# Three unused memory tiles shift where the operands of the weight products begin

## The chip, the core and the metric

The kernel runs on one core of a Trainium2 chip. The metric is the device time of one execution in microseconds (us), the median of several runs. The engines are named as in the profile: PE is TensorE with its matmuls, PEld its weight loads, DVE is VectorE, ACT is ScalarE, POOL is GpSimd, SP is SyncE, which issues the loads of the weights.

## What is computed

Two transformer blocks in float32 over 256 tokens with 1024 features, cut to what matters here:

```python
for l in range(DEPTH):                       # first block
    h = rmsnorm(x, norm_mix[l])
    proj = h @ w_in[l]
    ...                                      # two attention mixers: o_a, o_b
    mix = (jax.nn.sigmoid(gate_a) * (o_a @ w_branch_a[l])
           + jax.nn.sigmoid(gate_b) * (o_b @ w_branch_b[l]))
    x = x + mix @ w_out[l]
    h = rmsnorm(x, norm_mlp[l])
    x = x + jnp.square(jax.nn.relu(h @ w_mlp_in[l])) @ w_mlp_out[l]
...
for l in range(DEPTH):                       # second block
    f = swiglu(rmsnorm_2(x, ffn1_pre_g[l]), ffn1_w_gate[l], ffn1_w_up[l], ffn1_w_down[l])
    x = x + 0.5 * rmsnorm_2(f, ffn1_post_g[l])
    y = hybrid_mixer(...)                    # w_in_2, attention and mLSTM, w_out_2
    x = x + rmsnorm_2(y, mix_post_g[l])
    f = swiglu(rmsnorm_2(x, ffn2_pre_g[l]), ffn2_w_gate[l], ffn2_w_up[l], ffn2_w_down[l])
    x = x + 0.5 * rmsnorm_2(f, ffn2_post_g[l])
```

Nearly all arithmetic is in the products with the weight matrices. The mixers add small products, softmaxes and scans.

## The kernel before

**Products in three parts.** Every operand of a weight product is split into a high part (rounded to float32r, the one-pass float32 format of TensorE) and a low part (the rest). A product is then three matmuls: high by high, high by low and low by high. The activations live in pairs of tiles (`xh` and `xl`, `hT0` and `hT1`, `mT`, `mT2`, `mlT`, `attT`, `oaT`, `obT`), the weights in `hi` and `lo`.

**Stream of the weights.** `plan` lists all weight matrices in units of two k-tiles by up to 512 columns. `stream_dma` loads a unit into one of four `raw` buffers through SP's queue, five units ahead of its use. `stream_split` makes `hi` on ACT (line 249) and `lo` on DVE (line 250), two units ahead, into four buffers each. `load_unit` hands a unit to the product.

**Two forms of product.** A matmul has a stationary operand, of which 128 columns are loaded into the array (a weight load, PEld), and a moving operand, whose columns then stream through. The profile names the moving one first: `acc<-xh,hi` has `xh` moving and `hi` stationary.

- `gemm_feat` (lines 332, 334 and 335): 128 columns of the weights are stationary and all 256 tokens of the activations are moving. This is used for everything that gives features by rows: `w_in`, gate and up matrices, `w_mlp_in`, the branches.
- `gemm_tok` (lines 288, 289 and 290): 128 tokens of the activations are stationary and a whole weight row is moving, 512 columns, or 386 and 352 in two pieces of the `w_in` matrices. This is used for the down products (`hT`), the output products (`mT`, `mT2`) and the values.

Between the k-tiles of a product, `flush` issues small work of the mixers on PE. The order on ACT, DVE and PE comes from the scheduler, that on POOL and SP is the order of the code.

**Two places where another engine leads.** In the first mixer, `bias_job` writes a table to memory and reads it back through POOL's queue into `BT` (lines 554 to 561), and POOL then clears `gek` (line 716), for which the compressed keys wait. In the second mixer, `qkdone` sends each of six query and key pieces through two transfers and three POOL operations on 32 rows (lines 1212 to 1216), one piece behind the other, and the attention starts behind the last.

**Where the tiles lie.** Pools are laid out one behind the other from the left end of each partition, others from the right. Ahead of the large tiles lie a reserved piece of 16,384 bytes, four small constants of 128 bytes together, `ident` (512 bytes), `cols` (544) and `ones` (512): 18,080 bytes, which is 32 past a multiple of 128. All that follows inherits the 32. The small tiles of pool `st` end at 96 past such a multiple, and what follows them has 96, and so have most tiles of the right side. By the program's allocation, the operands of weight products begin as follows (bytes within a partition; in brackets, past a multiple of 128):

| tile | before | after the change |
|---|---|---|
| `xh`, `xl` | 34464, 42656 (32) | 34816, 43008 (0) |
| `hi`, first of four | 67232 (32) | 67584 (0) |
| `lo`, first of four | 83616 (32) | 83968 (0) |
| `hT0` | 110048 (96) | 110592 (0) |
| `mT0`, `mlT0` | 212960 (96) | 210944 (0) |
| `attT0` | 127712 (96) | 128256 (0) |
| `oaT0` | 177888 (96) | 178432 (0) |

Inside a tile, the slices that one matmul takes are 512 bytes apart (128 columns of the weights or tokens), 1024 (one k-tile of the activations), 2048 (one k-tile of 512 weight columns), or 1544 and 1408 (one k-tile of 386 and 352 columns).

Of the kernel before, what the change touches and what calls it, by code (L numbers as in the profile page):

```python
# [9 lines left out]
F32 = mybir.dt.float32  # L10
# [6 lines left out]
PSUM = bass.MemoryType.PSUM  # L17
DRAM = bass.MemoryType.DRAM
SIDE_R = "right"
# [9 lines left out]
FF2 = 2816  # L29
VIF = 386               # a quarter of the columns of the values, input and forget gates  # L30
SPLIT_AHEAD = 2         # weight units split ahead of their use
DMA_AHEAD = 5           # and loaded ahead of it


# ---------------------------------------------------------------- host layout
def widths_of(n):
# [3 lines left out]
class Wt:  # L40
    """A weight matrix cut into units of KT k-tiles by up to 512 columns, each unit contiguous."""

# [76 lines left out]

# constants of shape alone, [128, n] each  # L120
CONSTS = {}
# [73 lines left out]

# ---------------------------------------------------------------- the program
class Prog:
# [6 lines left out]

    # ---- weights
    def plan(self):
        """The order in which the column chunks of the weights are used."""
        o = [(W_IN1, c) for c in (4, 0, 1, 3, 2, 5, 6, 7, 8)]
        for c in range(2):
            o += [(W_BRB, c), (W_BRA, c)]  # L210
        o += [(W_OUT1, 0), (W_OUT1, 1)]
        o += [(W_MI, c) for c in range(8)] + [(W_MO, 0), (W_MO, 1)]

        def ffn(g, u, d):
            r = []
            for c in range(len(FFW)):
                r += [(g, c), (u, c)]
            return r + [(d, 0), (d, 1)]
        o += ffn(W_G1, W_U1, W_D1)
        o += [(W_IN2, c) for c in (6, 0, 1, 2, 3, 4, 5, 7, 8, 9, 14, 15, 16, 17, 10, 18, 12, 19, 11, 13, 20, 21)]  # L220
        o += [(W_ATT, 0), (W_ATT, 1), (W_MLB, 0), (W_MLB, 1), (W_OUT2, 0), (W_OUT2, 1)]
        o += ffn(W_G2, W_U2, W_D2)
        return [(W, c, u) for W, c in o for u in range(len(W.off[c]))]

    def stream_dma(self, upto):
        """Loads of the weights, up to a unit of the plan."""
        nc = self.nc
# [9 lines left out]
    def stream_split(self, upto):  # L237
        """High and low parts of the weights, up to a unit of the plan."""
        nc = self.nc
# [21 lines left out]

    # ---- work that waits for a place between the products
    def later(self, *fs):
# [10 lines left out]
    def gemm_tok(self, W, c, xh, xl, done, head=0, tail=0, mid=None, late=None, rate=1, delay=0, acc=None):  # L274
        """Token-major: accumulators [128 tokens, width], one per token tile; done(t, acc) when one is complete.
        In the first `head` and the last `tail` units token tile 0 goes ahead of tile 1; mid() comes before tile 1
        at the head, late(n) after each k-tile of tile 1 at the tail, n of them left."""
        nc = self.nc
# [41 lines left out]
    def gemm_feat(self, W, c, xh, xl, done, rate=1, delay=0):  # L320
        """Feature-major: accumulators [128, 2 feature tiles, 256 tokens]; done(i, acc)."""
        nc = self.nc
# [17 lines left out]

    # ---- small helpers
    def ptr(self):
# [14 lines left out]
    def split_one(self, src, k, ts, hi, lo, gcol=None, scale=None):  # L357
        """src(t, k) [128 tokens, 128], for the token tiles ts, transposed into hi/lo[:, k, :]."""
        nc = self.nc
# [14 lines left out]
    def split_T(self, src, ks, ts, hi, lo, gcol=None):  # L374
        """One job for the tensor engine per k-tile."""
        def job(k):
            return lambda: self.split_one(src, k, ts, hi, lo, gcol)
        return [job(k) for k in ks]
# [5 lines left out]
    def held(self, on):  # L384
        """What is traced inside queues behind the last split of activations, if `on`."""
        es = ExitStack()
        if on:
            for i in self.mark:
                es.enter_context(self.tc.issue_after(i.ins))
        return es  # L390

    def ssq(self, acc, src, scale=1.0):
        """acc [128,1] = sum of squares of src [128, n]."""
        nc = self.nc
# [4 lines left out]
    def newton_rsqrt(self, y, v, n, name):  # L399
        """y = v ** -0.5 on DVE."""  # L400
        nc = self.nc
# [12 lines left out]

    # ---- whole
    @contextmanager
    def banks(self, acc, tr, sm=0, o=0):
        """The PSUM banks of a phase."""
        with ExitStack() as es:
# [14 lines left out]
    def run(self):  # L434
# [9 lines left out]
        with ExitStack() as es:  # L444
# [16 lines left out]
            self.cols = self.cp.tile([128, 136], F32, name="cols")  # L461
            self.ones = self.cp.tile([128, 128], F32, name="ones")
            nc.scalar.dma_start(self.cols, ap["cols"])
            for c in range(4):
# [22 lines left out]
    def rows_rms(self, x, name):  # L487
        """Reciprocal root mean square of the rows of x: [128, 2]."""
        s = self.small(2, name + "_s")
# [8 lines left out]
    def along_free(self, rs, name):  # L498
        """rs [128, 2] by token laid along the free axis of every partition: [128, 256]; and the job for it."""
        nc = self.nc  # L500
# [10 lines left out]

    # ---- block 1: mixers
    def block1_mix(self, x0, x):
        tc, nc, ap, g = self.tc, self.nc, self.ap, self.g
        with ExitStack() as es, ExitStack() as rs_:
# [4 lines left out]
            ip = rpool("idx", 2)  # L520
            # keeps the tensor engine's clock up while the first loads are under way
            ps = self.psm()
# [13 lines left out]

            # position bias: BT[p, h, j] = table[bucket(128 + p - j), h], masked where the distance is negative
            tot = sum(CONSTS[n].shape[1] for n in C1)
# [8 lines left out]
            def bias_job():  # L547
# [3 lines left out]
                nc.vector.tensor_tensor(tv, ps[:16, :384], neg, op=ALU.add)  # L551
                # copies of the table in DRAM, read back with a shift by one from row to row
                tvd = self.dp.tile([16, 16, 384], F32, name="tvd")
# [8 lines left out]

            # projections
            qi = cp.tile([128, 2, 256], F32, name="qi")
# [46 lines left out]

            # indexer and top-k mask
            M = cp.tile([128, 2, 256], F32, name="M")
# [75 lines left out]

            # compressed keys and values  # L690
            kcT = cp.tile([128, 2, 16], F32, name="kcT")         # block diagonal over the two groups
            nc.gpsimd.memset(kcT, 0.0)
# [51 lines left out]

            # attention
            lp = rpool("att", 4)
# [18 lines left out]
            units = []  # L765
            for br in (1, 2, 0):        # 0: DSA; 1: slc; 2: win
                for t in (1, 0):
# [12 lines left out]
            def bm(U):  # L780
                """Position bias and top-k mask of a DSA unit's heads."""
                t, nh, h0 = U["t"], U["nh"], U["heads"][0]
# [55 lines left out]

            # compressed branch
            Lc = cp.tile([128, 2, 8, 16], F32, name="Lc")  # L840
# [70 lines left out]

            # gates
            gate = cp.tile([128, 16, 256], F32, name="gate")
# [52 lines left out]

    # ---- block 1: MLP, and the final norm
    def mlp(self, x1):
# [57 lines left out]
    def split_sb(self, h, hT, k):  # L1026
        """h [128, 2, 256] in SBUF into k-tiles k, k + 1 of hT."""
        nc = self.nc
# [27 lines left out]
    def down_post(self, W, hT, gi, x, mul, name, rs=None, gcol=None):  # L1056
        """x + mul * rmsnorm(h @ W * rs) * gain; starts on the transposed operand of the next layer (gain gcol)."""
        nc, tc = self.nc, self.tc
# [26 lines left out]
        def done0(t, ps):  # L1085
            square(0, t, ps)
            gained(0, t, ps)
            # loads the square root's table ahead of its use
            nc.scalar.activation(st[t][:, 3:4], sq[:, t:t + 1], AF.Sqrt)
# [58 lines left out]

    # ---- block 2: mixer
    def mixer2(self, x):  # L1150
        tc, nc, ap, g = self.tc, self.nc, self.ap, self.g
        xT, js = self.nextT
        with ExitStack() as es, ExitStack() as rs_:
# [40 lines left out]

            # attention projections
            qkp = rpool("qk", 1)
# [6 lines left out]
            def qkdone(i, gr):  # L1203
                def f(j, ps):
# [3 lines left out]
                    if j == 0:  # L1208
                        return
                    # rotation of the first 32 rows  # L1210
                    sw = rp.tile([32, 4, 256], F32, tag="sw", name="sw")
# [5 lines left out]
                return f  # L1217
            # input and forget gates of the mLSTM
            gif = gp.tile([128, 2, 8], F32, name="gif")
# [69 lines left out]

            # attention  # L1290
            lp = rpool("att2", 3)
# [67 lines left out]

            # values with a column of ones per head, and gates  # L1360
            mp = pool("ml", 1)
# [24 lines left out]

            # conv + silu on q and k of the mLSTM (feature-major)
            cw = self.cols[:, 56:120].rearrange("p (f j) -> p f j", f=16)
# [131 lines left out]

# ---------------------------------------------------------------- launch
# [14 lines left out]
```

## Time and profile before

| what | value |
|---|---|
| time, median of 3 runs | 1155.5 us (1154.68 to 1156.64) |
| profiled execution, first to last instruction (span) | 1152.0 us |
| mean granted TensorE clock | 0.992 |
| PE busy | 1125.9 us, 98% of the span |
| PEld busy | 1044.8 us, 91% |
| DVE, ACT, POOL busy | 732.2, 553.8 and 137.1 us |
| moved by the DMA engines | 197.03 MB, 171 GB/s in the mean |

The profiled execution has no other time than its span on record; the median of the runs lies 3.5 us above it, which is taken as what lies around the span. A busy PE means that a matmul is under way. It doesn't say how fast columns stream, since a matmul's end is modelled and neighbours overlap. What tells the pace is the distance from one matmul's start to the next one's.

### The profile page before, as it was taken

The numbers are of one execution on the slowest core, as the hardware profiler recorded it, in microseconds if no ns is written. First come the engines' busy times: TensorE is split into PE (matmuls) and PEld (weight loads), VectorE is DVE, ScalarE is ACT, GpSimd is POOL, SyncE is SP. The second block draws the span as 40 slices with busy tenths as digits, with TensorE's granted clock in tenths as the row PEclk, the third lists the DMA queues.
The fourth block names the chain that finished last, engine by engine and source line by source line (L and its number), as shares of the span: only waits on it lengthen the run. The fifth ranks groups of instructions, "written<-read, shape, count | busy, mean of one in ns | idle before, by whom it ended". The sixth has DMA issues, their size and how long they took to land.

```text
span 1152.0 us, 19495 instructions
## 1 busy us (share of the span) xinstructions
PE 1125.9 (98%) x7808; PEld 1044.8 (91%) x7808; DVE 732.2 (64%) x1155; ACT 553.8 (48%) x818; POOL 137.1 (12%) x141
## 2 busy tenths in 40 slices
PE   8988999999999999999999998999999999999997
PEld 8887899899988899999888998889999989999986
DVE  5755676766654466655547677556779776656553
ACT  6324454455544455444446334545555556444442
POOL 0411230000000000000000676000323000000000
PEclk9998999999999999999999999999999998999999
DMA  8783114555555556554654655444545565554662
GB/s 291 251 170 108 67 57 147 185 183 186 182 188 191 182 183 197 179 184 158 216 169 167 200 185 161 163 129 146 183 147 165 166 193 157 190 182 157 210 187 79
DMA packets 57035, 197.03 MB, mean 171 GB/s; under 512 B 6828, under 2 KB 7100, under 8 KB 56688
## 3 DMA queue, kind: packets, MB, share of 16 engines
q1 hardware_dynamic: 53856, 186.44, 49.4%
q0 software_dynamic: 2800, 9.21, 3.5%
q8 instruction: 61, 1.00, 0.3%
q14 instruction: 30, 0.25, 0.1%
q10 hardware_dynamic: 288, 0.14, 0.0%
HBM read 192.84 MB, written 1.44 MB: 169 GB/s over the span
## 4 chain that ended last, share of the span: by engine, by line
PE 85%; POOL 5%; DMA 4%; DVE 4%; issue 1%; ACT 1%; DVEq 0%; POOLq 0%; ACTq 0%
PE acc L332 16%; PE acc L334 16%; PE acc L335 16%; PE acc L290 9%; PE acc L289 9%; PE acc L288 9%; POOL sw L1215 2%; PE sm L795 2%; DMA sw<-qkT 2%; POOL qkT L1216 2%; DMA BT<-tvd 2%; PE o L828 1%; DVE lo L250 1%; POOL qkT L1214 1%; PE o L1337 1%
## 5 line engine op out<-in xcount | busy, mean ns | idle before, releaser
L250 DVE TENSOR_TENSOR lo<-raw,hi 128x1024 fp32r<-128x1024 f32 (+3 forms) x364 | 450.4, 1239 | 304.7 <-ACT hi L249 302.8
L249 ACT ACTIVATE hi<-raw 128x1024 fp32r<-128x1024 f32 (+3 forms) x364 | 372.9, 1025 | 452.8 <-PE acc L334 242.6
L332 PE MATMUL acc<-xh,hi 128*128 128x256 f32 x1656 | 471.1, 286 | 0.6 <-ACT hi L249 0.3
L334 PE MATMUL acc<-xl,hi 128*128 128x256 f32 x1656 | 471.3, 285 | 0.0
L335 PE MATMUL acc<-xh,lo 128*128 128x256 f32 x1656 | 469.4, 285 | 0.1
L332 PEld LDWEIGHTS acc<-xh,hi 128*128 128x128 f32 x1656 | 317.7, 192 | 4.5 <-issue 3.0
L334 PEld LDWEIGHTS acc<-xl,hi 128*128 128x128 f32 x1656 | 318.7, 192 | 2.4 <-issue 2.0
L335 PEld LDWEIGHTS acc<-xh,lo 128*128 128x128 f32 x1656 | 317.6, 192 | 1.6 <-issue 1.0
L290 PE MATMUL acc<-hi,hT 128*128 128x512 f32 x304 | 120.4, 396 | 0.0
L289 PE MATMUL acc<-lo,hT 128*128 128x512 f32 x304 | 120.2, 395 | 0.0
L288 PE MATMUL acc<-hi,hT 128*128 128x512 f32 x304 | 119.7, 396 | 0.0
L289 PEld LDWEIGHTS acc<-lo,hT 128*128 128x128 f32 x304 | 57.2, 188 | 13.7
L290 PEld LDWEIGHTS acc<-hi,hT 128*128 128x128 f32 x304 | 57.2, 188 | 13.7
L288 PEld LDWEIGHTS acc<-hi,hT 128*128 128x128 f32 x304 | 57.0, 188 | 13.4
L288 PE MATMUL acc<-hi,xh 128*128 128x386 f32 (+1 forms) x128 | 48.2, 378 | 0.9 <-ACT xh L366 0.9
L289 PE MATMUL acc<-lo,xh 128*128 128x386 f32 (+1 forms) x128 | 47.5, 371 | 0.0
L290 PE MATMUL acc<-hi,xl 128*128 128x386 f32 (+1 forms) x128 | 46.9, 372 | 0.2 <-DVE xl L367 0.2
L1034 POOL DMA_DIRECT2D row<-in_rows x4 | 2.3, 574 | 295.7 <-DVE xf L1017 216.8
L806 ACT ACTIVATE L<-L,nn 128x256 f32<-128x256 f32 (+1 forms) x48 | 21.2, 443 | 25.8 <-DVE nn L804 22.4
L288 PEld LDWEIGHTS acc<-hi,xh 128*128 128x128 f32 x128 | 24.0, 188 | 4.4 <-ACT xh L366 1.3
L290 PEld LDWEIGHTS acc<-hi,xl 128*128 128x128 f32 x128 | 24.0, 188 | 3.7 <-DVE xl L367 0.8
L289 PEld LDWEIGHTS acc<-lo,xh 128*128 128x128 f32 x128 | 24.1, 189 | 2.3
(414 smaller groups left out, 1263.1 us busy)
## 6 DMA issues: line engine op xcount, KB each, us to landing
raw<-in_w_in SPq DMA_DIRECT2D x100, 512.0 KB, 3.6
raw<-in_ffn_w_down SPq DMA_DIRECT2D x44, 512.0 KB, 4.4
raw<-in_ffn_w_gate SPq DMA_DIRECT2D x40, 512.0 KB, 3.5
raw<-in_ffn_w_up SPq DMA_DIRECT2D x40, 512.0 KB, 3.5
raw<-in_w_mlp_in SPq DMA_DIRECT2D x32, 512.0 KB, 3.5
raw<-in_w_mlp_out SPq DMA_DIRECT2D x32, 512.0 KB, 3.4
raw<-in_w_out SPq DMA_DIRECT2D x16, 512.0 KB, 3.6
raw<-in_w_in SPq DMA_DIRECT2D x16, 386.0 KB, 3.1
```

The source lines that it names most:

```text
L249: nc.scalar.activation(hi[:, :n * w], raw[:, :n * w], AF.Copy)
L250: nc.vector.tensor_tensor(lo[:, :n * w], raw[:, :n * w], hi[:, :n * w], op=ALU.subtract)
L288: nc.tensor.matmul(ps[t][:, :w], xh[:, k, sl], hi, start=(k == 0), stop=False)
L289: nc.tensor.matmul(ps[t][:, :w], xh[:, k, sl], lo, start=False, stop=False)
L290: nc.tensor.matmul(ps[t][:, :w], xl[:, k, sl], hi, start=False, stop=last)
L332: nc.tensor.matmul(o, hi[:, fs], xh[:, k, :], start=(k == 0 and f % 2 == 0), stop=False, skip_group_check=True)
L334: nc.tensor.matmul(o, hi[:, fs], xl[:, k, :], start=False, stop=False, skip_group_check=True)
L335: nc.tensor.matmul(o, lo[:, fs], xh[:, k, :], start=False, stop=last, skip_group_check=True)
L795: nc.tensor.matmul(ps[:, i, :], q[pr:pr + 64, U["fts"][i], t * 128:t * 128 + 128], kk, start=True, stop=True)
L806: nc.scalar.activation(L[:, i, :], L[:, i, :], AF.Exp, bias=nn[:, i:i + 1], scale=1.0, accum_out=lsum[:, t, br, h:h + 1])
L1215: nc.gpsimd.tensor_tensor(sw, sw, bc4(1), op=ALU.mult)
L1216: nc.gpsimd.tensor_tensor(q[0:32], q[0:32], sw, op=ALU.add)
```

## The change

Three tiles are added that nothing writes or reads: 352 bytes per partition behind `ones` in pool `const`, 2016 bytes at the right end in a pool of its own, and 192 bytes at the head of pool `st`. The first makes 18,080 bytes into 18,432, nine times 2048. The third brings the end of `st` to a multiple of 2048. The second moves all tiles of the right side. No instruction is added, removed or moved on any engine; only buffer numbers and addresses differ. The rest of the diff removes comments and docstrings.

```diff
@@ -460,6 +460,10 @@
             self.ident = self.cp.tile([128, 128], F32, name="ident")
             self.cols = self.cp.tile([128, 136], F32, name="cols")
             self.ones = self.cp.tile([128, 128], F32, name="ones")
+
+            self.cp.tile([128, 88], F32, name="pad_l")
+            pool("padr", 1, side=SIDE_R).tile([128, 504], F32, name="pad_r")
+            self.small(48, "pad_s")
             nc.scalar.dma_start(self.cols, ap["cols"])
             for c in range(4):
                 nc.sync.dma_start(x0[:, 2 * c:2 * c + 2, :], ap["xT"][:, 2 * c:2 * c + 2, :])
```

The second k-tile of a 386-column unit begins 1544 bytes into its tile, which is 8 past a multiple of 128 in both kernels when counted from the tile's start.

## Rows read from the trace of the kernel before

**Rows 1.** The page's shares of the chain of work that ended last, by engine.

```profile
PE 85%; POOL 5%; DMA 4%; DVE 4%; issue 1%; ACT 1%; DVEq 0%; POOLq 0%; ACTq 0%
```

**Rows 2.** The view of waits, of PE: who was waited for, us in total, times, longest us.

```profile
PE sm L726 <- DVE gek L717: 9.0, 1, 9.0
PE sm L1307 <- POOL qkT L1216: 3.0, 1, 3.0
```

**Rows 3.** PE's timeline in a stretch that holds only feature products from `xh` and `xl`: start in us, length, line, operands (the moving one first), shapes. Sixty-four intervals lie between the first and the last row.

```profile
251.80 0.28 PE L334 MATMUL acc<-xl,hi 128*128 128x256 f32 x1
251.92 0.28 PE L335 MATMUL acc<-xh,lo 128*128 128x256 f32 x1
...
259.48 0.28 PE L335 MATMUL acc<-xh,lo 128*128 128x256 f32 x1
```

**Rows 4.** The same of feature products from `mlT`. Twenty-two intervals lie between the first and the last row.

```profile
904.23 0.28 PE L334 MATMUL acc<-mlT,hi 128*128 128x256 f32 x1
...
906.83 0.28 PE L335 MATMUL acc<-mlT,lo 128*128 128x256 f32 x1
```

**Rows 5.** The same of a down product from `hT`: sixty-two intervals from the first row to the last.

```profile
329.72 0.39 PE L288 MATMUL acc<-hi,hT 128*128 128x512 f32 x1
329.95 0.40 PE L289 MATMUL acc<-lo,hT 128*128 128x512 f32 x1
...
344.19 0.39 PE L290 MATMUL acc<-hi,hT 128*128 128x512 f32 x1
```

**Rows 6.** The same of a value product of 512 columns from `xh`: four intervals from the first row to the last.

```profile
724.08 0.39 PE L288 MATMUL acc<-hi,xh 128*128 128x512 f32 x1
...
724.99 0.39 PE L289 MATMUL acc<-lo,xh 128*128 128x512 f32 x1
```

**Rows 7.** The same of a value product of 386 columns: six intervals from the first row to the last.

```profile
713.49 0.34 PE L289 MATMUL acc<-lo,xh 128*128 128x386 f32 x1
...
714.53 0.34 PE L289 MATMUL acc<-lo,xh 128*128 128x386 f32 x1
```

**Rows 8.** PE's timeline, two merged rows of small matmuls in plain float32, in which a moving column takes two cycles: twelve with 128 moving columns, and two with 257. The length runs from the first one's start to the last one's end.

```profile
753.92 1.50 PE L1337 MATMUL o<-v,PT 128*128 128x128 f32 x12
...
848.85 0.59 PE L1454 MATMUL o<-vm,w 128*128 128x257 f32 x2
```

**Rows 9.** The duration of a single one of these, by tile: count, ns (least, median, most), first and last start, forms.

```profile
L1337 PE MATMUL o<-v,PT x72: 270/275/377, 742.2 to 789.3; 128*128 128x128 f32 x72
...
L1454 PE MATMUL o<-vm,w x8: 377/378/380, 843.2 to 895.8; 128*128 128x257 f32 x8
```

**Rows 10.** PE's matmuls by line and form: operands, shapes, count, then busy us and mean ns of one, then idle time before them. The two other lines of each product have the same counts.

```profile
L332 PE MATMUL acc<-xh,hi 128*128 128x256 f32 x1648 | 469.1, 286 | 0.6 <-ACT hi L249 0.3 <-DVE x L959 0.2
...
L288 PE MATMUL acc<-hi,hT 128*128 128x512 f32 x304 | 119.7, 396 | 0.0
...
L288 PE MATMUL acc<-hi,xh 128*128 128x512 f32 x64 | 25.7, 401 | 0.0
...
L288 PE MATMUL acc<-hi,mT 128*128 128x512 f32 x64 | 25.3, 398 | 0.0
...
L288 PE MATMUL acc<-hi,xh 128*128 128x386 f32 x64 | 22.5, 355 | 0.9 <-ACT xh L366 0.9
```

**Rows 11.** The other feature products, from the view of line 332: operands, count, ns of one (least, median, most), first and last start, forms.

```profile
L332 PE MATMUL acc<-mlT,hi x64: 278/279/365, 903.4 to 926.6; 128*128 128x256 f32 x64
...
L332 PE MATMUL acc<-obT,hi x32: 279/279/363, 186.0 to 203.6; 128*128 128x256 f32 x32
...
L332 PE MATMUL acc<-oaT,hi x32: 279/279/363, 192.4 to 209.2; 128*128 128x256 f32 x32
...
L332 PE MATMUL acc<-attT,hi x32: 278/279/281, 890.8 to 903.1; 128*128 128x256 f32 x32
```

**Rows 12.** The chain that ended last in order of time, the ends of two stretches: start us, us, what.

```profile
62.51 6.29 DMA tvd<-tv
...
72.98 17.57 DMA BT<-tvd
634.81 5.13 DMA sw<-qkT
...
708.39 2.95 POOL qkT L1216
```

**Rows 13.** The instructions of line 332 in these two stretches: length, busy PE and PEld with counts, granted clock, DMA share, GB/s.

```profile
62.50:91.80 29.30, 10.78 (x37) 6.99 (x37) 0.88 0.92 172
634.80:711.30 76.50, 43.61 (x155) 29.57 (x154) 1.00 0.59 185
```

**Rows 14.** The view of waits, of ACT: us in total, times, longest us.

```profile
ACT hi L249 <- PE acc L334: 242.6, 140, 5.2
ACT hi L249 <- PE acc L290: 130.8, 83, 4.5
```

**Rows 15.** The splits of a full unit, by line and form.

```profile
L250 DVE TENSOR_TENSOR lo<-raw,hi 128x1024 fp32r<-128x1024 f32 x324 | 407.8, 1261 | 277.9 <-ACT hi L249 276.3 <-PE sm L363 0.5 <-PE acc L334 0.2
L249 ACT ACTIVATE hi<-raw 128x1024 fp32r<-128x1024 f32 x324 | 343.0, 1059 | 413.1 <-PE acc L334 218.1 <-PE acc L290 119.1 <-issue 48.9
```

**Rows 16.** The page's list of loads: tile and source, queue, count, KB each, median us to landing.

```profile
raw<-in_ffn_w_gate SPq DMA_DIRECT2D x40, 512.0 KB, 3.5
```

**Rows 17.** PE in a stretch of feature products alone: length, busy us of PE with count, granted clock, DMA share, GB/s.

```profile
250.00:300.00 50.00, 50.00 (x419) 1.00 0.58 190
```

## The prediction, made before the change was run

> **What bounds the kernel now.** I read the chain of work that ended last first: 85% of it is PE, and POOL and DMA have 9% together [rows 1]. PE's own waits are next: two are over a microsecond long and matter here, 9.0 us behind a POOL clear and 3.0 us behind a POOL rotation [rows 2]. So the time is PE's pace, except in two stretches that another engine leads. In order of time the chain shows these: a table's way through memory from 62.5 us until its last piece lands at 90.5, and six rotations one behind the other from 634.8 to 711.3 [rows 12].
>
> The pace is the distance between matmul starts. In a stretch of feature products it is (259.48 - 251.80) / 64 = 120.0 ns, the same from one row to the next [rows 3], at a granted clock of 1.00, the 2.4 GHz level [rows 17]. At one column a cycle 256 columns are 106.7 ns, so each matmul takes 13.3 ns more than its columns. In a down product 62 intervals give 233.4 ns [rows 5] for 512 columns, 213.3 ns of streaming: 20.1 more. A value product of 512 columns takes 0.91 / 4 = 227.5 ns [rows 6], 14.2 more, and one of 386 columns 1.04 / 6 = 173 [rows 7], 12 more. The extra hardly grows with the columns; it is a cost by matmul.
>
> Is it the operands' start? Two pairs of rows differ in an offset and little else. With the weights stationary at 32, `xh` moving at 32 gives 120.0 [rows 3] and `mlT` moving at 96 gives 2.60 / 22 = 118.2 [rows 4]. With the weights moving at 32, `xh` stationary at 32 gives 227.5 [rows 6], `hT` at 96 gives 233.4 [rows 5]. No product in this trace has an operand at 0, so what happens there is an extrapolation.
>
> The small products in plain float32 bear on it from another side: their columns take two cycles each. Two of them with 257 columns start 0.59 - 0.378 = 0.212 us apart [rows 8, 9], and 514 cycles are 0.214: no extra, though they are just as far off a boundary. An extra that vanishes when operands are fetched at half the rate looks like a limit of the fetch, which a partly used first and last piece would reach and a clean start not. That is why I take the alignment as the likelier cause. Twelve with 128 columns start (1.50 - 0.275) / 11 = 111.4 ns apart [rows 8, 9], above their 106.7 ns of streaming. Such matmuls are as close as weight loads of 128 columns let them be, as far as rows show, so 111.4 is the floor that I take for a feature product.
>
> **The change part by part.** Nothing is issued that was not issued before, so the sum is matmuls by the change of their pace.
>
> 1. Feature products from `xh` and `xl`: 3 x 1648 = 4944 [rows 10]. Those in the two stretches led by others gain nothing: there, line 332 has 37 and 155 records [rows 13]; three lines make 111 and, with the few missing records, 480 (five pieces of 96). The remaining 4353 go from 120.0 to 111.4: 8.6 ns each, 37.4 us.
> 2. Feature products from `mlT`, `obT`, `oaT` and `attT`: 3 x (64 + 32 + 32 + 32) = 480 [rows 11], from 118.2 to 111.4: 3.3 us.
> 3. Down and output products: 3 x (304 + 64) = 1104 [rows 10], from 233.4 to 215. That is the 213.3 of streaming and 1.7 for what the rows round away: 20.3 us.
> 4. Value products of 512 columns: 192 [rows 10], from 227.5 to 215: 2.4 us. Of 386 columns: 192 [rows 10], but three quarters of them run behind the rotations and change nothing; 48 from 173 to 162 give 0.5 us. Half of these keep an offset of 8, which may cost them this.
> 5. Where the other engines lead, what PE saves becomes waiting: some 480 x 8.6 ns = 4.1 us and 144 x 11 ns = 1.6 us are added to the 3.0 us at line 1307. Not counted above, so not taken off again.
> 6. Softmax and norm chains on DVE and ACT lose cover as the products around them shrink. The rows have hardly any wait of PE on them; I take off 2 us, of a possible 0 to 6.
>
> Sum: 37.4 + 3.3 + 20.3 + 2.4 + 0.5 - 2 = 61.9 us. From the profiled span of 1152.0 that leaves 1090; the median lies 3.5 us above the span, so about **1094 us**.
>
> At nothing I cost: the splits, 1.06 us on ACT and 1.26 on DVE for a unit [rows 15] that PE uses for 24 matmuls, 2.88 us now and 2.67 at 111.4 ns; ACT waits for PE, 373 us in all [rows 14], not PE for ACT. The loads: 3.5 us to landing [rows 16], asked for five units ahead; at the faster pace 190 GB/s [rows 17] would become 204. If that cover went, PE would wait at the start of units. The small float32 products: no extra to lose by rows 8 and 9, and none to gain.
>
> From both sides: the best that alignment can do is pure streaming, 106.7 and 213.3. Then the terms are 57.9 + 5.5 + 22.2 + 2.7 + 0.6 - 2 = 86.9 us, and the time is 1069. The worst is the third rival below. I take 111.4 because it is the nearest row of PE with nothing else in the way.
>
> The Trainium skill, page TensorE: Matmul & The Clock Gate, section Back-to-back issue gap, gives columns / 2.4 plus 2.5 ns for matmuls in a row at the full clock. This would be 109.2 and 215.8 ns where the rows show 120.0 and 233.4; by it the sum is an estimated 71 us and the time 1084. The trace doesn't agree before the change, so the page either leaves the offset out or doesn't hold for these operands.
>
> **The rivals.**
>
> *Partial.* The extra has another cause, and the offset only modulates it: each class falls to the best pace that the trace already has. Feature products 120.0 to 118.2, 4353 x 1.8 ns = 7.8 us; down and output products 233.4 to 227.5, 1104 x 5.9 ns = 6.5 us. Time 1141. For it: those are the only effects of an offset that rows show. Against it: half-rate products have no extra at all.
>
> *No effect.* The extra is what a weight load takes from the stream in this format, whatever the addresses: 1155.5 us. For it: the extra is about the same for 256, 386 and 512 columns, as one load each would make it. Against it: the pairs of rows above. It would come out this way too if offsets counted only in small pieces of which 32 and 96 are multiples. The Trainium skill, page SBUF — State Buffer, section Specifications (TRN2), has 16-byte lines in this memory; by that rule the time stays 1155.5. The two pairs of rows speak against it, since offsets of 32 and 96 would then be alike.
>
> *Slower.* The cost of the stationary operand grows with its offset up to the next boundary, and a multiple of 128 counts as the full 128, not as 0. From 32 to 96 the stationary operand costs 5.9 more and the moving one 1.8 less [rows 3 to 6]. Half as far again that is +8.9 and -2.7, so +6.2 ns against `xh` now: 4353 x 6.2 = 27.0 us, 480 x 8.0 = 3.8, 1104 x 0.3 = 0.3, 192 x 6.2 = 1.2; the rotations' 480 x 6.2 = 3.0 are covered by the wait there. Time 1188. It decides from a feature pace over 120.0; each ns above costs 4.4 us. For it: the slope between 32 and 96 is real. Against it: a clean start makes fewer pieces to fetch, not more.
>
> **How the numbers follow.** The main case (at least half of the extra above the floors goes) has 50% and spans 1069 to 1125. Partial: 17%, 1125 to 1152. No effect: 14%, within 2.3 us, which is 0.2%, about what a measurement of this kernel can tell from no change. Slower: 19%, 1158 to 1190. So faster 0.67, same 0.14, slower 0.19. A range of 1070 to 1160 leaves out most of the slower case and a few per cent below. That the tiles don't land where intended is not a case: their starts are the program's.
>
> **What would show it.** Right: starts of feature matmuls near 0.111 us apart instead of 0.120, of down products near 0.215 instead of 0.233, in every stretch and from its first unit on; the wait at line 1307 grown from 3.0 to 8 or 9 us; the stretch from 634.8 to 711.3 as long as before. Partial: 0.118 and 0.227. Wrong: starts 0.120 apart with both operands at 0, or further; or the new pace with PE waiting for `hi` or `lo` at the units, where the cover was misjudged. If the feature pace lands at 0.107 to 0.109, the floor taken from the small products was too high and the time is near 1070 to 1085.

## The result and the profile after

| | before | after |
|---|---|---|
| time, median | 1156.07 us (1154.68 to 1157.92, 4 runs) | 1145.49 us (1144.71 to 1146.21, 4 runs) |
| span of the profiled execution | 1152.0 us | 1144.4 us |
| mean granted TensorE clock | 0.992 | 0.991 |
| PE busy | 1125.9 us | 1117.1 us |

The ratio is 0.9915 with a 95% interval of 0.9894 to 0.9936: faster by 10.6 us, where 61.9 were forecast. The time lies inside the range of 1070 to 1160 us only because that range was drawn to hold the rivals; the main case was to end at 1125 at the latest. The order of the work is the same, 7808 matmul records in both profiles.

PE's timeline of the kernel after, in the stretch that [rows 3] show of before. There are again sixty-four intervals from the first row to the last:

```profile
251.79 0.28 PE L332 MATMUL acc<-xh,hi 128*128 128x256 f32 x1
251.91 0.28 PE L334 MATMUL acc<-xl,hi 128*128 128x256 f32 x1
...
259.47 0.28 PE L334 MATMUL acc<-xl,hi 128*128 128x256 f32 x1
```

That is 7.68 / 64 = 120.0 ns, to the digit what it was. The largest term of the sum, 37.4 us, is not there at all. The same view of feature products from `mlT`, twenty-seven intervals, to be held against [rows 4]:

```profile
899.08 0.28 PE L335 MATMUL acc<-mlT,lo 128*128 128x256 f32 x1
...
902.32 0.28 PE L335 MATMUL acc<-mlT,lo 128*128 128x256 f32 x1
```

3.24 / 27 = 120.0 ns, where it was 118.2: these became slower. And a down product from `hT`, sixty intervals, against [rows 5]:

```profile
328.22 0.39 PE L290 MATMUL acc<-hi,hT 128*128 128x512 f32 x1
...
341.83 0.39 PE L290 MATMUL acc<-hi,hT 128*128 128x512 f32 x1
```

13.61 / 60 = 226.8 ns instead of 233.4. Only here is something won: 1104 x 6.6 ns = 7.3 us. The 480 products from `mlT`, `obT`, `oaT` and `attT` lose 480 x 1.8 ns = 0.9 us.

The view of waits of PE after, for [rows 2]; all lines of the code stand four further down:

```profile
PE sm L730 <- DVE gek L721: 11.1, 1, 11.1
PE sm L1311 <- POOL qkT L1220: 1.2, 1, 1.2
```

And the chain that ended last, in the two stretches of [rows 12]: start us, us, what.

```profile
71.59 19.90 DMA BT<-tvd
...
631.67 4.35 DMA sw<-qkT
...
703.47 2.97 POOL qkT L1220
```

The table lands at 91.49 us, 0.9 later than before, and the rotations take 631.67 to 706.44, 74.8 us instead of 76.5. With the two pace terms this makes -7.3 + 0.9 + 0.9 - 1.7 = -7.2 us, against -7.6 in the two spans. The medians differ by 3 us more than the two spans; a single profile of each doesn't tell where these are.

### The profile page after: what moved, and what is told of

Same layout as the page of the kernel before. It is cut to its first block, busy times and chain, and to the rows that moved or that the text cites. A ratio compares the mean times of both kernels' runs of the same rounds, so it can differ in the third digit from the quotient of the medians.

```text
span 1144.4 us, 19495 instructions
## 1 busy us (share of the span) xinstructions
PE 1117.1 (98%) x7808; PEld 1042.9 (91%) x7808; DVE 733.1 (64%) x1155; ACT 553.6 (48%) x818; POOL 137.0 (12%) x141
## 4 chain that ended last, share of the span: by engine, by line
PE 84%; POOL 5%; DMA 5%; DVE 4%; ACT 1%; issue 1%; DVEq 0%; POOLq 0%; ACTq 0%
PE acc L332 16%; PE acc L334 16%; PE acc L335 16%; PE acc L288 9%; PE acc L290 9%; PE acc L289 9%; DMA BT<-tvd 2%; PE sm L799 2%; POOL sw L1219 2%; POOL qkT L1220 2%; DMA sw<-qkT 2%; PE o L832 1%; POOL qkT L1218 1%; DVE lo L250 1%; PE o L1341 1%
## 5 line engine op out<-in xcount | busy, mean ns | idle before, releaser
L290 PE MATMUL acc<-hi,hT 128*128 128x512 f32 x304 | 118.5, 390 | 0.0
L289 PE MATMUL acc<-lo,hT 128*128 128x512 f32 x304 | 118.3, 389 | 0.0
L288 PE MATMUL acc<-hi,hT 128*128 128x512 f32 x304 | 117.7, 389 | 0.0
```

The costliest lines, as they stand in the source:

```text
L288: nc.tensor.matmul(ps[t][:, :w], xh[:, k, sl], hi, start=(k == 0), stop=False)
L289: nc.tensor.matmul(ps[t][:, :w], xh[:, k, sl], lo, start=False, stop=False)
L290: nc.tensor.matmul(ps[t][:, :w], xl[:, k, sl], hi, start=False, stop=last)
```

## The experiments

Four theories stood at one time or another. **A**, the prediction's: a clean start makes an operand cheaper. **O**: each operand's own offset counts. **D**: the distance between the starts of the moving and the stationary operand counts, first put modulo 128 bytes and after the first four runs modulo 256. **L**: a pair of addresses can run at one of two paces, and the moment of entry chooses.

A distance is counted here as the start of the moving operand less that of the stationary one, so that 192 is the same as 64 the other way round.

The paces quoted for whole kernels are the mean interval from one matmul's start to the next one's of the same class, over the whole trace, with intervals above 130 ns (256 columns) or 245 ns (512) left out as interruptions. So counted, before has 119.9 (features from `xh`), 117.8 (other features) and 233.4 (down and output), after has 119.9, 119.9 and 226.9.

**The pace by itself, for pairs of offsets.** The tiles of this probe begin 128 past a multiple of 256; offsets are counted from there.

```python
COMBOS = [(m, s, 256, 128) for s in (0, 32, 64, 96) for m in (0, 16, 32, 48, 64, 80, 96, 112)]
...
for i in range(48):
    o = s // 4 + 128 * (i % 4)
    nc.tensor.matmul(acc[:k, :n], stat[:, o:o + k], mov[:, m // 4:m // 4 + n], start=(i == 0), stop=(i == 47))
nc.tensor.matmul(sep, one, one, start=True, stop=True)
```

> This kernel leaves out the whole computation: it runs only series of 48 float32r matmuls in a row on one weight slice of 2048 columns, and writes something of the right shape. Each series has a moving operand that begins m bytes past a multiple of 128 and a stationary one that begins s bytes past (256 or 512 moving columns). Theory D (only the distance m - s, modulo 128, counts): 0/0 and 32/32 and 96/96 alike, near 120.0 ns (256 columns) and 226.7 (512); 64/0, 0/64, 96/32, 32/96 alike, near 117.8 for 256 and 233.3 for 512. Theory O (each operand's own offset counts): s = 96 gives 233 for 512 whatever m is, and m = 96 gives 118 for 256 whatever s is, so 96/96 stands out. Theory A (a clean start is cheaper): 0/0 is the fastest of all. Series with 32, 64 or 96 stationary columns: if the extra over pure streaming (13.3 ns) is taken by the weight load, it falls to about 3, 7 and 10 ns; if it is a fixed cost by matmul, it stays at 13.

PE's timeline of this run: the first eight pairs, the stationary operand at 0 and the moving one at 0, 16, ... 112. A row of 48 is one series; its length holds 47 intervals and one duration.

```profile
12.13 6.00 PE L50 MATMUL acc<-mov,stat 128*128 128x256 f32 x48
...
18.11 5.95 PE L50 MATMUL acc<-mov,stat 128*128 128x256 f32 x48
...
24.03 5.84 PE L50 MATMUL acc<-mov,stat 128*128 128x256 f32 x48
...
29.85 5.93 PE L50 MATMUL acc<-mov,stat 128*128 128x256 f32 x48
...
35.75 5.69 PE L50 MATMUL acc<-mov,stat 128*128 128x256 f32 x48
...
41.42 6.00 PE L50 MATMUL acc<-mov,stat 128*128 128x256 f32 x48
...
47.40 6.01 PE L50 MATMUL acc<-mov,stat 128*128 128x256 f32 x48
...
53.38 5.74 PE L50 MATMUL acc<-mov,stat 128*128 128x256 f32 x48
```

Equal starts (6.00) are among the slowest, and 64 (5.69) and 112 (5.74) are the fastest; at 64 each matmul takes (6.00 - 5.69) / 47 = 6.6 ns less. The steady paces, from the starts of the 11th to the last matmul of each series, for 256 moving columns:

| stationary \ moving | 0 | 16 | 32 | 48 | 64 | 80 | 96 | 112 |
|---|---|---|---|---|---|---|---|---|
| 0 | 120.0 | 118.7 | 116.6 | 118.4 | 113.3 | 120.1 | 119.9 | 113.4 |
| 32 | 118.4 | 117.1 | 120.0 | 118.6 | 117.8 | 118.4 | 117.8 | 120.1 |
| 64 | 113.4 | 119.2 | 118.3 | 117.2 | 120.0 | 116.7 | 116.6 | 118.3 |
| 96 | 118.8 | 119.4 | 113.3 | 119.1 | 118.3 | 117.1 | 120.0 | 118.6 |

The diagonal is 120.0 throughout: A falls, and so does O as it was put ahead of this run, with 96, 96 standing out. Pairs of one distance are not all alike off the diagonal, though: at distance 64 the table has 113.3 and 117.8. Moved by 128 the pace is 118.6, by 256, 512 or 1024 it is 120.0 again: the period is 256 bytes, not 128. With 512 moving columns it is the other way round: 226.6 to 226.7 on the whole diagonal, 228.8 for two pairs at +64, and 230.9 to 234.3 for all others. With 32 stationary columns instead of 128 the equal starts give 113.3 for 256 columns, but 231.6 for 512.

**All operands at one offset, or `hT` alone moved to it.** Two runs on whole kernels, designed when D was still thought to repeat after 128 bytes:

```diff
 (e_all96, against before)
+            self.cp.tile([128, 16], F32, name="pad_l")
+            self.small(16, "pad_s")
 (e_ht32, against before)
+            self.small(16, "pad_s")
```

> The kernel before with two other unused pieces, so that every operand of a weight product begins 96 past a multiple of 128: none is aligned, all distances are 0. Theory D: the time and the paces of the changed kernel, 120.0 ns for every feature product and 226.7 for every 512-column product, about 1145.5 us, ratio to before 0.991. Theory O: feature products at 118, every 512-column product at 233; 1149 us. Theory A: nothing is gained, 1156 us.

> The kernel before with 64 unused bytes at the head of the pool of small tiles alone: xh, xl, hi and lo stay at 32, hT moves from 96 to 32, and so do attT, oaT and obT; mT, mT2 and mlT stay at 96. Theories D and O: 912 down-product matmuls go from 233.4 to 226.7, -6.1 us, 288 feature products from 117.8 to 120, +0.6: 1150.5 us, ratio 0.995. Theory A: no change, 1156 us.

Ratios 0.9994 (0.9975 to 1.0013) and 0.9988 (0.9971 to 1.0006): no change. Down products from `hT` in the first, PE's timeline, sixty-three intervals:

```profile
328.50 0.39 PE L290 MATMUL acc<-hi,hT 128*128 128x512 f32 x1
...
343.14 0.39 PE L290 MATMUL acc<-hi,hT 128*128 128x512 f32 x1
```

14.64 / 63 = 232.4 ns. Modulo 128 `hT` and `hi` were alike, modulo 256 they were 128 apart in both runs; the first probe has 118.6 instead of 120.0 at that distance for 256 columns, and the probe further down 232.3 for 512, as here. `mT`, which in the first run was at distance 0 modulo 256 too, ran at 227.0 there. D as first put was wrong in its period, and the miss gave it.

**Distance 0 without any alignment.** The decisive pair. `hT` alone is brought to distance 0, then all operands, each 160 past a multiple of 256, where not one begins on a multiple of 64:

```diff
 (e_ht0, against before)
+            self.small(48, "pad_s")
 (e_rel0, against before)
+            pool("padr", 1, side=SIDE_R).tile([128, 16], F32, name="pad_r")
+            self.small(48, "pad_s")
```

> The kernel before with 192 unused bytes ahead of the small tiles, so that hT, attT, oaT and obT begin 160 past a multiple of 256, as hi and lo do, instead of 224; no operand comes to a multiple of 32 more than before. Theory D (distance modulo 256): down products 233.4 to 226.7 ns, 912 x 6.7 = 6.1 us less; 288 feature products from attT, oaT and obT 117.8 to 120.0, 0.6 us more; feature products from xh stay 120.0, mT and mT2 233.4. Ratio 0.995. Theory A (a clean start is what made the changed kernel faster): no pace moves, ratio 1.000.

> The same, and 64 unused bytes on the right side: every operand of a weight product begins 160 past a multiple of 256, none on a multiple of 64 even. Theory D: all paces are those of the changed kernel (226.7 for hT, mT and mT2, 120.0 for all feature products), ratio 0.9915 to 0.995 as there. Theory A: the paces of before, ratio 1.000.

Ratios 0.9939 (0.9914 to 0.9963) and 0.9947 (0.9928 to 0.9965). Down products of the second, sixty-nine intervals:

```profile
326.32 0.40 PE L288 MATMUL acc<-hi,hT 128*128 128x512 f32 x1
...
341.98 0.39 PE L288 MATMUL acc<-hi,hT 128*128 128x512 f32 x1
```

15.66 / 69 = 227.0 ns. The other paces are those of the changed kernel as well: 119.9 for `xh`, 119.8 for the other features. In `e_ht0` the class that was left at distance 192, `mT` and `mT2`, kept its 233.4. So the changed kernel's gain is had with no operand on a boundary, and A falls for good. The ratio of 0.9947 is nearer to the 7.3 - 0.9 = 6.4 us of the pace terms (0.9945) than the 0.9915 of the changed kernel; the two intervals share 0.9928 to 0.9936.

**`xh` away from `hi`.** If distance 0 is among the slowest for feature products, then the change left the largest class where it hurts. Two runs move `xh` and `xl` by 64, below `hi` at 128 and above `hi` at 0:

```diff
 (e_x64, against after)
             self.xtp = pool("xT", 1)
...
+            px.tile([128, 16], F32, name="px")
+            py.tile([128, 16], F32, name="py")
 (e_x64b: py 48 instead of 16)
```

The pools `px` and `py` lie ahead of and behind pool `xT`.

> The changed kernel with 64 unused bytes ahead of xh and xl and 64 behind them, so that these two begin at 64 past a multiple of 128 and all other operands stay at 0. Theory D: feature products from xh and xl go from 120.0 to 117.8, 4353 x 2.2 ns = -9.6 us, the 240 value products from xh or xl that count from 227 to 233, +1.4: 1137 us, ratio to before 0.984. Theory A: worse than the changed kernel or the same, 1145.5 or more. Theory O says nothing of 64.

> The changed kernel with 64 unused bytes ahead of xh and 192 behind xl: xh and xl begin 64 past a multiple of 256, hi, lo, hT, mT and all others at 0. Theory D: feature products from xh at 113.3 to 117.8 ns instead of 120.0, hT and mT at 226.7. If 113.3 everywhere, 4353 x 6.7 = 29 us below the changed kernel, ratio 0.967; if 117.8 in most places, as in the run with xh at 64 and hi at 128, 1131 us, ratio 0.980 less 1 us for mT and mT2. Theory L: the same mixture of 113.3 and 117.8 by stage as in that run. Theory A: xh is off its clean start, the paces are those of before for these, ratio 0.99 to 1.00.

Ratios 0.9804 (0.9776 to 0.9832) and 0.9876 (0.9850 to 0.9902). The first did a little better than the 0.984 that D as first put gave, the second worse than both its figures, 0.967 and 0.980. Of the 9.5 us between the two profiled spans, 1129.3 and 1138.8, 6.3 fall between the 4680th and the 4940th matmul, where the rotations took 75.5 us in the first run and 79.2 in the second; the feature products from `xh` and `xl` are nearly alike, 116.3 and 116.9 ns in the mean. The view of three stretches of feature products of the first: length, busy us of PE with the count of matmuls, granted clock, DMA share, GB/s.

```profile
275.00:300.00 25.00, 25.00 (x215) 1.00 0.57 183
450.00:500.00 50.00, 50.00 (x444) 1.00 0.61 195
980.00:1030.00 50.00, 50.00 (x427) 1.00 0.60 188
```

And of the second:

```profile
450.00:500.00 50.00, 50.00 (x427) 1.00 0.58 189
980.00:1030.00 50.00, 50.00 (x426) 1.00 0.61 189
625.00:650.00 25.00, 25.00 (x223) 1.00 0.65 202
```

And one of the kernel after:

```profile
450.00:500.00 50.00, 50.00 (x419) 1.00 0.58 186
```

419 in 50 us is 120.0 ns, 427 is 117.8, 444 is 113.3 (the count has two or three matmuls that cross an edge). One kernel, one pair of starts modulo 256, and two paces: a stage of hundreds of matmuls stays in the one that it fell into. This half of L is shown. What chooses the pace is not: within such a stage the result tiles and the buffers of `hi` and `lo` change again and again while the pace stays, so it is not these, but that it is the moment of entry is only argued.

**Which distances have two paces.** The probe again, five series for each pair, each behind a small float32 matmul of another width (two earlier forms of it, with four operand tiles and with three and six series for each pair, gave no result):

> The whole computation is left out: PE runs only series of 24 float32r products of 256 moving and 128 stationary columns. Counted past 128, modulo 256, the moving operand begins at 0, 16, ... 240 and the stationary one at 0, and seven more pairs lie off that grid; each pair has five series, each behind a small float32 matmul of another width (34 to 128 columns), so that they are entered at another moment. Sixteen last series have 512 moving columns. Theory D (the distance of the two starts, modulo 256, sets the pace): 120.0 ns at distance 0, 113.3 at 64 and 112; pairs of one distance are alike, so (64, 0), (192, 128) and (128, 64) would be; with 512 columns 226.7 at distance 0 and 231 to 233.4 elsewhere. Theory L (a pair of addresses has two locked states, 113.3 and 117.8, and the moment of entry chooses): at 64 the five series differ among themselves, some 113.3 and some 117.8; a pair that gives 113.3 in all five would be the better one for the kernel. With a single state per pair, L falls.

PE's timeline, the five series at distance 64:

```profile
74.09 3.07 PE L50 MATMUL acc<-mov,stat 128*128 128x256 f32 x24
...
77.14 3.07 PE L50 MATMUL acc<-mov,stat 128*128 128x256 f32 x24
...
80.19 3.07 PE L50 MATMUL acc<-mov,stat 128*128 128x256 f32 x24
...
83.24 2.97 PE L50 MATMUL acc<-mov,stat 128*128 128x256 f32 x24
...
86.19 2.97 PE L50 MATMUL acc<-mov,stat 128*128 128x256 f32 x24
```

Some series are 0.10 us shorter over 23 intervals than others of the same addresses, 4.4 ns each. The steady paces, from the starts of the 7th to the last matmul:

| moving, stationary (past 128, modulo 256) | distance | five series, ns |
|---|---|---|
| 0, 0 | 0 | 120.0 in all five |
| 64, 0 | 64 | 117.8, 117.8, 117.8, 113.4, 113.4 |
| 192, 128 | 64 | 117.7, 113.3, 113.4, 113.4, 113.3 |
| 96, 32 | 64 | 117.7 to 117.8 in all five |
| 0, 64 | 192 | 113.4, 117.8, 113.4, 117.8, 113.4 |
| 192, 0; 64, 128; 128, 192 | 192 | 113.3 to 113.4 in all |
| 112, 0 | 112 | 114.1 to 114.5 in all five |

The other distances on the grid of 16 give 116 to 120.2, with a single 113.3 at 16, and 104 and 120, which are no multiples of 16, 119.8 to 130.5. D holds for 0, where one pace is all that was seen. Two paces show at 64 and 192, and several among the five series at some other distances too: 113.3, 116.5 and 118.7 at 16, 118.4 and 120.1 at 128. Whether the starts count beside the distance is open at 64, since 96, 32 ran at 117.7 to 117.8 in all six series of the two probes. The starts of `e_x64`, 64 and 128 past a multiple of 256, are the pair 192, 0 of this table: 113.3 to 113.4 in all five series, yet 117.8 in most stages of that kernel; five series were too few to see its second pace. With 512 columns distance 0 is again the fastest, 227.9 in this short series, and the rest 228.8 to 236.8.

**The better version.** `xh` and `xl` go 112 past `hi`, everything else stays at distance 0:

```diff
 (e_x112, against after; e_x112b has px 24 and leaves pad_r at 504)
-        return (self.xtp.tile([128, 8, 256], F32R, tag="xh", name="xh"),
-                self.xtp.tile([128, 8, 256], F32R, tag="xl", name="xl"))
+        return tuple(self.xtp.tile([128, 2112], F32R, tag=n, name=n)[:, 4:2052].rearrange("p (k n) -> p k n", k=8)
+                     for n in ("xh", "xl"))
...
+            px.tile([128, 56], F32, name="px")
+            py.tile([128, 40], F32, name="py")
-            pool("padr", 1, side=SIDE_R).tile([128, 504], F32, name="pad_r")
+            pool("padr", 1, side=SIDE_R).tile([128, 472], F32, name="pad_r")
```

> The changed kernel with xh and xl at 240 past a multiple of 256, and hi, lo, hT, mT and all others at 128: distance 112 for the feature products from xh, 0 for the down and output products. Theory D with one state at 112, as the five series of 114.1 to 114.5 ns have it: the feature products from xh go from 120.0 to 114.4 in every stage, 4353 x 5.6 = 24 us less than the changed kernel; the 192 value products of 512 columns, whose distance becomes -112, from 227 to 233, 1.2 us more. Ratio 0.971. Theory L for every pair (what runs before a stage chooses among states at 112 too): 118 to 120 in some stages, ratio 0.975 to 0.99.

> The same distances with other starts: xh and xl at 112, all others at 0 past a multiple of 256. Theory D: as the run with 240 and 128, within 0.3%, ratio 0.971. Theory O (the start itself counts beside the distance, as for (64, 0) against (96, 32)): a pace other than 114.4, up to 120.0 and a ratio of 0.992.

Medians 1126.59 and 1127.54 us against 1154.94 of the kernel before: ratios 0.9766 (0.9737 to 0.9795) and 0.9762 (0.9735 to 0.9789). By these ratios both beat the changed kernel too, and the two choices of starts don't differ. The same three stretches of the first:

```profile
275.00:300.00 25.00, 25.00 (x223) 1.00 0.64 195
450.00:500.00 50.00, 50.00 (x444) 1.00 0.60 194
980.00:1030.00 50.00, 50.00 (x444) 1.00 0.63 192
```

Here every long stage is at 113.3, better than the 114.4 of the short series. In the stages of the mixers, where small products interrupt, means over 50 us lie between 113.8 and 117.0; over the whole trace the mean is 113.9. Yet the ratio fell short of 0.971. The waits and the rotations of this run show a part of the reason:

```profile
PE sm L1315 <- POOL qkT L1224: 6.4, 1, 6.4
PE sm L734 <- DVE gek L725: 5.2, 1, 5.2
...
PE acc L289 <- DVE lo L250: 1.4, 1, 1.4
```

```profile
71.66 13.57 DMA BT<-tvd
...
613.14 4.49 DMA sw<-qkT
...
689.73 2.34 POOL qkT L1224
```

The start of the 4680th of the 7808 matmuls, in the midst of the rotations, was 21.5 us earlier than in the profile of the changed kernel, that of the 4940th, behind them, only 12.7 us, and the last one's 22.0. POOL and the transfers, which lead there, took 78.9 us instead of 74.8, and PE waited 6.4 us for them instead of 1.2. Of these 5.2 us more, 4.1 are the longer rotations; only about 1 us is PE's gain that became waiting. Another 1.4 us went into a wait for `lo` in the same stretch. In `e_x112b` and `e_x64b` the rotations were as long, 78.8 and 79.2 us, with the same wait of 6.4 us. Why they took longer wasn't tested.

The other way round, a part of the gain is not PE's pace: the table landed at 85.2 us instead of 91.5, and PE waited for `gek` 5.2 us instead of 11.1. In the four kernels with `xh` moved the table lands between 85.2 and 88.5 us, in the six others between 89.4 and 93.0; the reason wasn't tested.

## Why the prediction was wrong

1. **The step that failed** is the answer to "Is it the operands' start?". Two pairs of rows were read as effects of an offset past a multiple of 128. In both pairs the distance of the two operands changes as well: modulo 256, `xh`, `hi` and `lo` began at 160, `hT`, `mT` and `mlT` at 224. The four paces of [rows 3 to 6] are those of distances 0, 64, 192 and 0, and the change brings the starts of all these tiles to distance 0. Read so, the same rows give 120.0 to 120.0, 118.2 to 120.0 and 233.4 to 227.5, in all -6.5 + 0.9 us. The first probe has 226.7 and 233.4 for 512 columns at distances 0 and 192. `e_rel0` and the diagonal of the first probe show that this reading is the right one.
2. **Term 1** (37.4 us): 0. The feature products stayed at 120.0, since `xh` and `hi` were at distance 0 before and are still. The floor of 111.4, read from float32 matmuls with 128 columns, was reached in no run: 113.3 is the fastest steady pace. Distance 0 is among the slowest with 256 columns; `e_x112` took 6 ns from each by leaving it.
3. **Term 2** (3.3 us): -0.9, of the wrong sign, by the same rule.
4. **Term 3** (20.3 us): 7.3. The class was right, the floor wrong: 215 was streaming alone, and in no run did 512 columns go below 226.6.
5. **Term 4** (2.9 us): nothing. The value products run from `xh`, at distance 0 already: 229.1 ns before and 229.5 after by the mean over the trace. Two counts were off as well, worth under 1 us: of the 192 products of 386 columns 96 start between 634.8 and 711.3 us, not three quarters, and of the 480 feature products 464, the others ahead of that stretch; no records are missing there.
6. **Terms 5 and 6**: no test in the changed kernel, since the feature products beside the rotations kept their pace and saved nothing that could have become waiting. In `e_x112`, where they ran faster, the wait at the rotations grew by 5.2 us, but 4.1 of them are the longer rotations, which step 5 had taken as unchanged; about 1 us bears it out. No new wait of softmax or norm chains was over 2 us.
7. **The float32 rows.** That an extra vanishes at half the rate was read as a limit of the fetch; no run here tests that. That a clean start would be free of it did not follow. For this premise the trace had no row, and the text called it an extrapolation and gave it half of the chance all the same.
8. **The rivals.** *Partial* (1141 us) came nearest. Its second half was right in size, 6.5 us for the down and output products against 7.3, and by luck: it took the value products' pace as the best of their kind, and these happened to be at the distance to which the change brought the others. Its first half, 118.2 for all feature products, was not. *No effect* and *Slower* each hold for one class: nothing for `xh`, slower for `mlT`. The Trainium skill, page SBUF — State Buffer, section Specifications (TRN2), has lines of 16 bytes; all starts of the first probe are multiples of 16, and its paces lie between 113.3 and 120.1, so that rule alone doesn't tell the pace. By the page TensorE: Matmul & The Clock Gate, section Back-to-back issue gap, of the same skill, 256 columns would take an estimated 109.2 ns and 512 an estimated 215.8. The section has this formula for a single matmul and not for the stream of weight loads and matmuls that runs here; the fastest that any run here shows are 113.3 and 226.6.

What causes the dependence on the distance is argued, not shown. PEld is busy 91% of the span, so the next weights are read while columns stream, and with 32 stationary columns in place of 128 the equal starts lose their extra 6.7 ns: that fits two reads in each other's way. The 512-column series, where equal starts are the best and fewer stationary columns are slower, do not follow from so simple a picture.

## What to carry to other kernels

When a pace differs between two kinds of products, list the start of both operands and their difference before blaming either; two rows that differ in an offset can differ in a distance too, as here. Give float32r products with 256 moving columns a moving tile that begins 112 bytes past the stationary one, modulo 256, and those with 512 columns a distance of 0, and measure the pace in each stage, since some distances have two. Here they gave 113.3 ns against 120.0, and 226.9 against 233.4. A gain of PE's pace is only kept where PE leads; the stretches led by another engine must be looked at again afterwards.

## What was not expected of the hardware

- The pace depends on the distance of the two starts modulo 256 bytes: 113.3 to 120.2 ns for 256 columns and 226.6 to 236.8 for 512 on the grid of 16 bytes, at the full granted clock, and distance 0, the fastest for 512 columns, is among the slowest for 256.
- At distances 64 and 192 the same addresses run at 113.3 or at 117.8, and a long stage of hundreds of matmuls keeps one of them; what chooses it is open. At 112 long stages all settle at 113.3.
- The steady paces of equal starts and of the fastest pairs, 113.3, 120.0 and 226.7, are 272, 288 and 544 cycles of 2.4 GHz, all multiples of 16.
